# A diffusion layer on one core: one staging tile in another pool, the gate rows loaded earlier, and the mixer's modulation on six tiles with GpSimd and ScalarE beside VectorE

## The chip, the core and the metric

The kernel runs on one core of one Trainium2 chip. The core has TensorE (PE, with its weight loads shown as PEld), VectorE (DVE), ScalarE (ACT), GpSimd (POOL) and SyncE (SP), each with its own instruction stream that runs in order. The metric is the device time of one execution in microseconds. Lower is better.

## The reference

One layer of a diffusion backbone, batch 1, with 256 latent tokens (`LAT`) and 256 context tokens (`CTX`), width 2048, all in float32. The part that matters here:

```python
mod_l = (silu_c @ w_mod[l] + b_mod[l]).reshape(B, N_MOD, D_MODEL)     # 9 modulation vectors of 2048
mod_c = (silu_cc @ w_mod[l] + b_mod[l]).reshape(1, N_MOD, D_MODEL)
xl = half_step_ffn(xl, mod_l, 0, g_norm[l, 0], w_ffn1_up[l], w_ffn1_down[l])   # vectors 0, 1, gate 2
xc = half_step_ffn(xc, mod_c, 0, g_norm[l, 0], w_ffn1_up[l], w_ffn1_down[l])
hl = adaln(xl, g_norm[l, 1], mod_l, 3)                                          # vectors 3, 4
hc = adaln(xc, g_norm[l, 1], mod_c, 3)
# mixer: projections of hl and hc, attention (8 heads, 2 KV heads) and a bidirectional mLSTM (8 heads)
xl = xl + mod_l[:, 5, None, :] * mixer_output(att_l, hm_l, m_l[3], m_gain[l], w_out[l])  # gate 5
xl = half_step_ffn(xl, mod_l, 6, g_norm[l, 2], w_ffn2_up[l], w_ffn2_down[l])    # vectors 6, 7, gate 8
return rms_norm(xl, g_final)

def half_step_ffn(x, mod, i, g, w_up, w_down):
    h = adaln(x, g, mod, i)                       # rms_norm(x, g) * (1 + mod[i+1]) + mod[i]
    a, b = jnp.split(h @ w_up, 2, axis=-1)
    return x + 0.5 * mod[:, i + 2, None, :] * ((jax.nn.silu(a) * b) @ w_down)
```

A modulation vector is a product of one row (the condition) with a 2048 x 2048 weight. `w_mod` has nine of those, 16.8 MB each.

## The kernel before

**Products.** Every float32 weight tile of 128 x 2048 (1 MB) is split into two rounded halves: `hi` by ACT (L102, 128x1024 each) and `lo` by DVE (L103, weight minus `hi`). A product is then three matmuls, `hi*hi`, `hi*lo`, `lo*hi` (`mm3`, L124 to L126). The weight tiles `raw` have three buffers, `hi` and `lo` four of half a tile, that is, two tiles.

**First FFN.** Eleven blocks of 512 hidden columns (`NB`). After the first, each up block is a 2x2 block product by seven products instead of eight (`quad`). Sums of weight tiles that it needs are made by accumulating DMAs into `chain` tiles. Each of the seven has two steps (columns), so a quad has 14 steps of 24 matmuls or more; a step calls `after(step)`. The gated result `ca` is transposed, copied by ACT with a minus sign into a tile `stg` (L670) and stored to HBM by SP (`hid`, L671). `stg`, `ca`, `c12`, `cy`, the two `sraw` tiles and the condition tile `cBh` lie in the pool `f1u`, which is given back after the up products; the pool `f1` with the sums `acc`, the difference tiles and the gate tiles (tag `two`, two buffers) takes its place. `chain` lies in the pool `ch`, which lives until the mixer.

**Down products.** Blocks are taken in pairs (`pair`), again as seven products of two steps each; the last block is done alone (`last1`). In the last pair `through_gate` multiplies finished columns of `acc` by the gate row, vector 2 broadcast over the partitions (L853), and an accumulating DMA of POOL adds the residual. `both_gates` loads the gate rows of both sequences for one column block (L858); they are loaded in the step of their use, for the second, fifth, sixth and seventh product. `last1` loads one gate row per column block and sequence in the same way.

**Modulation.** Vectors 0 and 1 are made on PE at the start. The others are made in units: a unit is a tile of 128 x 1024 weights (0.52 MB, output index on the partitions) times the condition broadcast over the partitions, summed along the row by the same DVE instruction (`mod_half`, L183). A vector has 32 units. `mod_items` paces them: before unit `n` as many steps must have passed as the interpolated `pace` says, plus two (`WAIT`) after each load of a condition half. Vectors 2 to 4 (96 units, two DVE instructions each, for both sequences) run beside the up products of the first FFN. Vectors 5 to 7 (96 units, latent tokens alone) run beside the mixer's projections, in `mod_late`, with two tiles `sraw` that SP loads; vector 8 runs in the second FFN. A step of the mixer is one call of `next(beside["part"])`: one per 128 input rows in `products_of`, one per four in `channels`.

**Mixer.** Weights in order: `w_c`, `w_a`, `w_b` (values and gates), eight `w_mk` heads, eight `w_mq` heads, `w_kv`, `w_q0`, `w_o0`, `w_o1`, `w_q1`, then `w_out`. `conv` (L1168, L1175) follows each head. `latents` builds for each head the masks `E` and the scaled queries `A`; `heads_out` makes `hm`. GpSimd's only products in tiles are `gm` (L1383).

**Order.** The order on each engine is made by a planner from the program order, the dependencies and its estimates; instructions marked by `keep_in_program_order` keep their order among each other. So the same program step may stand earlier or later in another build.

Of the kernel before, what the change touches and what calls it, by code (L numbers as in the profile page):

```python
# [9 lines left out]
F32 = mybir.dt.float32  # L10
F32R = mybir.dt.float32r
BF16 = mybir.dt.bfloat16
# [36 lines left out]
def tile_layer(ctx: ExitStack, tc: tile.TileContext, I: dict, out: bass.AP):  # L49
# [106 lines left out]
    class Conditions:  # L156


        def __init__(self, half, load, at):
            self.half, self.load, self.at = half, load, at  # L160
# [81 lines left out]
    def mod_late(sp, i0, i1, pace):  # L242

        cB = sp.tile([P, 1024], F32, name="cBl", bufs=1)
        cond = Conditions(lambda h: h, lambda h: conditions({LAT: cB}, h, h + 1, (LAT,)), lambda h: {LAT: cB})
        raws = lambda: sp.tile([P, 1024], F32, tag="sraw", name="sraw", bufs=2)
        return mod_items(half_items(i0, i1), nc.sync.dma_start, raws, 2, cond, None, pace)

    def mod_end(i, seqs):

# [51 lines left out]
    def steps(it, n=1):  # L302
        for _ in range(n):
            next(it, None)
# [268 lines left out]
    with pool(name="f1u", bufs=1) as f1u:  # L573
# [87 lines left out]
        def turned():  # L661

            if not turn:
                return
            n, t, ca = turn.pop(0)
            tb = tbank()
            for j in range(FB):
                nc.tensor.transpose(tb[:, j * P : (j + 1) * P], ca[:, j * P : (j + 1) * P], ident)
            stg = f1u.tile([P, CB], F32, tag="stg", name="stg")
            nc.scalar.activation(stg, tb, AF.Copy, scale=-1.0)  # L670
            nc.sync.dma_start(hidd[n][:, t].rearrange("p j c -> p (j c)"), stg)  # L671

# [3 lines left out]
        def c12_tile():  # L676
            return f1u.tile([P, CB], F32, tag="c12", name="c12", bufs=2)
# [84 lines left out]

        halves = [cBh[:, q, :] for q in range(2)]
        cond = Conditions(lambda h: h, lambda h: conditions(halves, h, h + 1), lambda h: halves)
        side = mod_items(half_items(2, 5), nc.sync.dma_start, sraw, 2, cond, lambda: c12_tile().bitcast(BF16), ((96, (NB - 2) * 14 + 2),))

        def first_steps(step):
            if step in (1, 2, 3, 4, 5, 6):
# [86 lines left out]
    def both_gates(cb, seqs=(CTX, LAT)):  # L855
        g = two("gate")
        for s in seqs:
            nc.sync.dma_start(g[:, s, :], mod_rows[2][s, cb * CB : (cb + 1) * CB].partition_broadcast(P))  # L858
        return g

    NP = (NB - 1) // 2

    def pair(p):

        X, Y, Z, ra, gates = {}, {}, {}, {}, None
        w = lambda m, cb: I["w_dn1"][2 * p + m, cb]

        def put(t, cb, b, first=False):
            if first and p == 0:
                nc.scalar.activation(col(t, cb), b, AF.Copy)  # L870
            else:
                nc.vector.tensor_tensor(col(t, cb), col(t, cb), b, op=ALU.add)

        def through_gate(t, cb):

            if p < NP - 1:
                return
            s, tt = divmod(t, 2)
            half_gated(col(t, cb), col(t, cb), gates[:, s, :], -1.0 if cb % 2 else 1.0)
            accum(col(t, cb), xsrc[s][tt * P : (tt + 1) * P, cb * CB : (cb + 1) * CB])  # L880

        def c11x(c, s):
            put(2 * s, 2 * c, X[c, s], True)

        def c11z(c, s):
            put(2 * s, 2 * c, Z[c, s])
            through_gate(2 * s, 2 * c)

        def p5(c, s):
            put(2 * s + 1, 2 * c + 1, Y[c, s], True)  # L890

        def p35(c, s):
            put(2 * s, 2 * c + 1, Y[c, s], True)

# [12 lines left out]

        def loaded(m, cb):
            raw = raw_tile()
            nc.sync.dma_start(raw, w(m, cb))  # L910
            return raw

        def again(c):
            if p + 1 < NP:
                nc.sync.dma_start(chain_[c], I["w_dn1"][2 * p + 2, 2 * c])

        def b22(c):
            ra[c] = loaded(1, 2 * c + 1)
            return ra[c]

        held = lambda c: chain_[c]

        order = (
            ("a11", held, X, True, lambda c: accum(chain_[c], w(0, 2 * c + 1)), c11x, None),
            ("a12", lambda c: loaded(1, 2 * c), Z, True, None, c11z, 0),
            ("n1", held, Y, True, lambda c: accum(chain_[c], w(1, 2 * c + 1)), p5, None),
            ("s4", b22, Y, False, lambda c: accum(ra[c], w(0, 2 * c + 1)), p35, None),
            ("s2", held, X, False, lambda c: accum(chain_[c], w(1, 2 * c)), c12, 1),
            ("s3", lambda c: ra[c], X, False, None, x3, 1),
            ("a22", held, Y, True, again, c21, 0),  # L930
        )
        todo = first_plan if p == 0 else plan if p < NP - 1 else last_plan
        for m, (g, src, dst, fresh, then, use, gate) in enumerate(order):
            a = place0[m] if p == 0 and m < 2 else place[g]
            for c in range(2):
                wt = split(src(c))
                if then:
                    then(c)
                for x in todo.get(2 * m + c, "").split():
                    if x.startswith("raw"):  # L940
                        hid_load(2 * p + 2 + int(x[3]), raws[int(x[3])])
                    else:
                        make[x]()
                if p == NP - 1 and gate is not None:
                    gates = both_gates(2 * c + gate)
                for s in range(2):
                    if fresh:
                        dst[c, s] = tbank() if c and dst is not X else bank()
                    for j in range(FB):
                        k = slice((FB * s + j) * P, (FB * s + j + 1) * P)  # L950
                        mm3(dst[c, s], a[:, 0, k], a[:, 1, k], *wt(slice(j * CB, (j + 1) * CB)), fresh and j == 0, j == FB - 1, True)
                    use(c, s)
# [20 lines left out]
    def last1():  # L973

        norm = iter(())
        kept = {}
        for s in (CTX, LAT):
            for n, cb in enumerate((1, 3, 0, 2) if s == CTX else (2, 0, 3, 1)):
                c = slice(cb * CB, (cb + 1) * CB)
                wt = kept.pop(cb, None) or load_split(I["w_dn1"][NB - 1, cb])  # L980
                if s == CTX and n >= NCB - 2:
                    kept[cb] = wt
                g = both_gates(cb, (s,))[:, s, :]
                for t in range(2 * s, 2 * s + 2):
                    b = bank()
                    block_products(b, wt, t)
                    a = acc[:, t, c]
                    y = f1.tile([P, CB], F32, tag="xr", name="y", bufs=1)
                    half_gated(y, b, g)
                    nc.vector.tensor_tensor(a, a, y, op=ALU.add)  # L990
                    if s == LAT:
                        nc.sync.dma_start(x1d[(t - 2) * P : (t - 1) * P, c], a)
                    if n == 0:
                        ss1[t] = sm.tile([P, 4], F32, tag="ss4", name="ss4", bufs=4)
                    sumsq(ss1[t][:, cb : cb + 1], a)
                    steps(norm, (1, 0, 0, 0, 2, 2, 2, 2)[2 * n + t % 2])
            drain(norm)
            norm = adaln(s)
        return norm
# [32 lines left out]
    with ExitStack() as mx:  # L1032
# [21 lines left out]

        mmcm = pool(name="mm", bufs=1)

        beside["part"] = mod_late(mmcm.__enter__(), 5, 8, ((45, 44), (75, 96), (96, 160)))
        ev_mv(6, 0, b_c)
        b_a = {}
        drain(project("w_a", 416, range(4), b_a))  # L1060
# [13 lines left out]
        def gates():  # L1074
# [35 lines left out]
            for d in range(2):  # L1110
# [15 lines left out]
                nc.vector.tensor_tensor_scan(Mq, uq, uq, m3, ALU.max, ALU.max)  # L1126
                nc.vector.tensor_copy(hc[:, d, 4 + a : 5 + a], m2)
                nc.vector.tensor_tensor(hc[:, d, 4 + z : 5 + z], m2, btT[:, d, 2 + a : 3 + a], op=ALU.add)
            negM = one([NH, 2, T], "negM")
            nc.vector.tensor_scalar(negM, MT.rearrange("h d t q -> h d (t q)"), -1.0, None, op0=ALU.mult)  # L1130
            nc.sync.dma_start(negMd, negM)

# [26 lines left out]


        mkT = one([P, NH, T], "mkT")
        mqT = one([P, NH, T], "mqT")
        C1 = one([P, NH, 2, 130], "C1")

        def conv(b, ch, ns):
# [12 lines left out]
        def state(h, kTc):  # L1178
# [3 lines left out]
                nc.tensor.transpose(tb[:, t * P : (t + 1) * P], kTc[:, t * P : (t + 1) * P], ident)  # L1182
            kn = m1.tile([P, 2, P], F32, tag="kn", name="kn", bufs=1)
            nc.scalar.activation(kn, tb[:, :256].rearrange("p (t d) -> p t d", t=2), AF.Copy)
            vw = m1.tile([P, 2, 2, 130], F32, tag="vw", name="vw", bufs=1)
            for t in range(2):
                for d in range(2):
                    nc.vector.tensor_scalar(vw[:, t, d, :], v1[CTX][:, t, h, :], wg[:, t, d, h : h + 1], None, op0=ALU.mult)
# [36 lines left out]
            todo.append((h, y))  # L1225


        hm = one([P, 2, 1024], "hm")
        ready = [0]

# [551 lines left out]
```

## Time and profile before

| | |
|---|---|
| median of 3 runs | 2760.77 us (2759.16 to 2763.49) |
| the profiled execution | 2753.58 us |
| its span | 2751.9 us |
| mean granted TensorE clock | 0.986 |
| HBM traffic | 234 GB/s over the span |
| modulation units beside the mixer | 96, the first at 1453, the last at 1851 us |
| `lo` splits (L103) of `raw` weights, 128x1024 mostly | 600 of 1205 ns |

Times in the trace are microseconds from the start of the span. A group's line gives its instructions, busy time and mean; an idle engine's time is put down to what ended its wait. The profiled execution is 7.2 us below the median of the timed runs, so differences are worked out against the profile and then carried over to the median.

### The profile page before, as it was taken

What the parts mean: (1) busy time and instruction counts of PE and PEld (TensorE: products, weight loads), DVE (VectorE), ACT (ScalarE), POOL (GpSimd) and SP (SyncE); (2) the same over time, 40 slices, a digit from 0 to 9 for tenths busy, and PEclk for the clock granted to TensorE, in tenths of its full rate; (3) what the DMA queues carried; (4) which work ended last, traced back from release to release, by engine and by line L of the source; (5) the groups of instructions that cost most, each with busy time, mean ns of one, the idle gap of its engine ahead of it and who ended that gap; (6) DMA issues with size and microseconds to landing.
All of it is one profiled execution on the core that took longest, in us unless ns stands there. A gap on an engine that the chain in (4) does not pass through costs nothing. (4 is left out here: it accounts for less than half of the span.)

```text
span 2751.9 us, 33080 instructions
## 1 busy us (share of the span) xinstructions
PE 2647.2 (96%) x12573; PEld 2180.0 (79%) x12573; DVE 1995.5 (73%) x2740; ACT 1263.4 (46%) x1586; POOL 174.6 (6%) x217
## 2 busy tenths in 40 slices
PE   6999999999999889999999998999999999999998
PEld 3588878887878768888789788877898888888886
DVE  2387778778877778888786789797685666666657
ACT  3454444544444455444363335345474444444444
POOL 0000000110000000000210000111000000000000
PEclk8999999999999999999999999999999999999999
DMA  8879999999999969889966766574466666666553
GB/s 349 313 233 249 246 274 277 263 269 268 269 254 266 269 193 239 224 233 219 227 220 217 257 236 234 178 259 161 163 230 227 216 228 223 217 225 225 211 190 132
DMA packets 125887, 645.32 MB, mean 235 GB/s; under 512 B 13464, under 2 KB 17560, under 8 KB 68256
## 3 DMA queue, kind: packets, MB, share of 16 engines
q1 hardware_dynamic: 106144, 513.18, 51.7%
q0 software_dynamic: 19584, 130.03, 24.1%
q8 instruction: 99, 1.62, 0.2%
q14 instruction: 60, 0.49, 0.0%
HBM read 627.36 MB, written 15.79 MB: 234 GB/s over the span
## 5 line engine op out<-in xcount | busy, mean ns | idle before, releaser
L103 DVE TENSOR_TENSOR lo<-raw,hi 128x1024 fp32r<-128x1024 f32 (+3 forms) x600 | 720.3, 1205 | 399.7 <-ACT hi L102 388.4
L102 ACT ACTIVATE hi<-raw 128x1024 fp32r<-128x1024 f32 (+3 forms) x600 | 625.2, 1045 | 796.4 <-PE mm L126 644.5
L125 PE MATMUL mm<-lo,hhi 128*128 128x512 f32 (+3 forms) x1024 | 392.5, 383 | 15.1 <-DVE lo L103 15.0
L124 PE MATMUL mm<-hi,hhi 128*128 128x512 f32 (+3 forms) x1024 | 394.2, 388 | 4.4 <-ACT v L1053 4.4
L126 PE MATMUL mm<-hi,hlo 128*128 128x512 f32 (+3 forms) x1024 | 391.0, 382 | 0.0
L102 ACT ACTIVATE hi<-chain 128x1024 fp32r<-128x1024 f32 x240 | 251.8, 1058 | 264.7 <-PE mm L126 129.5
L103 DVE TENSOR_TENSOR lo<-chain,hi 128x1024 fp32r<-128x1024 f32 x240 | 289.3, 1220 | 98.0 <-ACT hi L102 96.5
L183 DVE SCALAR_TENSOR_TENSOR c<-sraw,cBh 128x1024 bf16<-128x1024 f32 x192 | 229.3, 1218 | 36.8 <-DMA sraw<-in_w_mt 33.5
L124 PE MATMUL mm<-hi,h2hi 128*128 128x512 f32 x640 | 249.1, 389 | 0.0
L125 PE MATMUL mm<-lo,h2hi 128*128 128x512 f32 x640 | 249.0, 389 | 0.0
L126 PE MATMUL mm<-hi,h2lo 128*128 128x512 f32 x640 | 249.0, 389 | 0.0
L125 PEld LDWEIGHTS mm<-lo,hhi 128*128 128x128 f32 x1024 | 195.8, 191 | 51.3 <-DVE lo L103 19.8
L124 PEld LDWEIGHTS mm<-hi,hhi 128*128 128x128 f32 x1024 | 194.5, 190 | 36.6 <-ACT v L1053 4.8
L126 PEld LDWEIGHTS mm<-hi,hlo 128*128 128x128 f32 x1024 | 195.3, 191 | 34.0
L183 DVE SCALAR_TENSOR_TENSOR sraw<-sraw,cBl 128x1024 f32<-128x1024 f32 x128 | 155.6, 1220 | 44.9 <-DMA sraw<-in_w_mt 42.0
L124 PE MATMUL mm<-hhi,hi 128*128 128x512 f32 (+1 forms) x384 | 142.0, 371 | 1.2 <-ACT hi L102 1.2
L124 PEld LDWEIGHTS mm<-hi,h2hi 128*128 128x128 f32 x640 | 120.1, 188 | 25.2
L125 PEld LDWEIGHTS mm<-lo,h2hi 128*128 128x128 f32 x640 | 120.1, 188 | 24.8
L126 PEld LDWEIGHTS mm<-hi,h2lo 128*128 128x128 f32 x640 | 120.1, 188 | 24.8
L126 PE MATMUL mm<-hhi,lo 128*128 128x512 f32 (+1 forms) x384 | 137.9, 361 | 1.2 <-DVE lo L103 1.2
L124 PE MATMUL mm<-hi,hid2h 128*128 128x512 f32 x352 | 138.5, 395 | 0.0
L125 PE MATMUL mm<-hlo,hi 128*128 128x512 f32 (+1 forms) x384 | 138.4, 361 | 0.0
(377 smaller groups left out, 4719.3 us busy)
## 6 DMA issues: line engine op xcount, KB each, us to landing
sraw<-in_w_mt SPq DMA_DIRECT2D x224, 512.0 KB, 5.3
raw<-in_w_up2b SPq DMA_DIRECT2D x80, 1024.0 KB, 4.7
raw<-in_w_dn SPq DMA_DIRECT2D x70, 1024.0 KB, 4.8
chain<-in_w_up1b POOLq DMA_DIRECT2D x60, 1024.0 KB, 11.0
raw<-in_w_up1b SPq DMA_DIRECT2D x40, 1024.0 KB, 8.8
mraw<-in_w_m SPq DMA_DIRECT2D x32, 1024.0 KB, 8.0
chain<-in_w_dn POOLq DMA_DIRECT2D x30, 1024.0 KB, 9.3
chain<-in_w_up1b SPq DMA_DIRECT2D x20, 1024.0 KB, 7.1
```

The source lines that it names most:

```text
L102: nc.scalar.activation(hi, src, AF.Copy)
L103: nc.vector.tensor_tensor(lo, src, hi.bitcast(F32), op=ALU.subtract)
L124: nc.tensor.matmul(out_ap, sh, mh, start=first, stop=False, skip_group_check=skip)
L125: nc.tensor.matmul(out_ap, sh, ml, start=False, stop=False, skip_group_check=skip)
L126: nc.tensor.matmul(out_ap, sl, mh, start=False, stop=last, skip_group_check=skip)
L183: ins = nc.vector.scalar_tensor_tensor(junk() if junk else raw, raw, 1.0, cB[s], op0=ALU.mult, op1=ALU.mult, accum_out=mT[:, i, s, kt, h : ...
```

## The change

Four edits, made together:

1. `stg` moves from `f1u` to `chp`, the pool of `chain`. The tile `y` of `last1`, which had a place in `f1`, uses the same place.
2. The pace of vectors 2 to 4 is `(NB - 2) * 14 - 8` = 118 steps instead of 128 for its 96 units.
3. In the last pair the gate rows are loaded at listed steps (`GATES`), and the sixth product uses the rows of the fifth again; in `last1` the rows of column block `i + 2` are loaded while block `i` is done, into four half tiles.
4. In the mixer the class `Beside` replaces `mod_late`: three tiles of its own and three more that are free until the queries are made (two halves of the place of `mqT`, and the place of `rt`). Units 0 to 71 are "early", and every other of them is multiplied in place by GpSimd and summed by an ACT copy with accumulation; the others stay one DVE instruction. The first six fetches are issued by POOL, all later ones by ACT, one step after a unit's product on DVE or two after one on GpSimd. The pace is 72 units in 54 steps and the other 24 by step 150, instead of 45 in 44, 75 in 96 and 96 in 160. To make room, `negM` shares a place with `nM`, `vw` with `E`, and `mqT` is allocated after the early units are finished.

```diff
+    class Beside:
+        def __init__(self, sp, i0, i1, early, n_early, pace):
...
+            for x in [sp.tile([P, 1024], F32, name=f"sr{j}", bufs=1) for j in range(3)]:
+                self.fetch(x, False, nc.gpsimd)
+            for x in early:
+                self.fetch(x, True, nc.gpsimd)
+        def fetch(self, x, early, queue):
+            if self.asked >= (self.n_early if early else len(self.items)):
+                return
+            i, kt, h = self.items[self.asked]
+            pin(queue.dma_start(x, I["w_mt"][i - 2, kt, :, h * 1024 : (h + 1) * 1024]))
...
+        def one(self):
+            i, kt, h = self.items[self.n]
+            x, early = self.slots[self.n]
+            if self.n < self.n_early and self.n % 2:
+                pin(nc.gpsimd.tensor_tensor(x, x, self.cB, op=ALU.mult))
+                self.due.append((self.done + 2, self.n, True))
+            else:
+                mod_half(x, {LAT: self.cB}, None, i, (LAT,), kt, h)
+                self.due.append((self.done + 1, self.n, False))
+            self.n += 1
+        def finish(self, n, add):
...
+            if add:
+                pin(nc.scalar.activation(x, x, AF.Copy, accum_out=mT[:, i, LAT, kt, h : h + 1]))
+            self.fetch(x, early, nc.scalar)
...
-            stg = f1u.tile([P, CB], F32, tag="stg", name="stg")
+            stg = chp.tile([P, CB], F32, tag="stg", name="stg")
...
-        side = mod_items(half_items(2, 5), ..., ((96, (NB - 2) * 14 + 2),))
+        side = mod_items(half_items(2, 5), ..., ((96, (NB - 2) * 14 - 8),))
...
+    LAST = [(CTX, cb) for cb in (1, 3, 0, 2)] + [(LAT, cb) for cb in (2, 0, 3, 1)]
+    def last_gate(i):
+        if i % 4 in (0, 2) and len(last_gates) < 4:
+            g = two("gate")
+            last_gates.extend((g[:, 0, :], g[:, 1, :]))
+        if i < len(LAST):
+            s, cb = LAST[i]
+            nc.sync.dma_start(last_gates[i % 4], mod_rows[2][s, cb * CB : (cb + 1) * CB].partition_broadcast(P))
...
+        GATES = {0: 0, 1: 2, 4: 1, 5: 3, 11: 0, 12: 2}
...
-                if p == NP - 1 and gate is not None:
-                    gates = both_gates(2 * c + gate)
+                if p == NP - 1:
+                    if (2 * m + c) in GATES:
+                        ahead.append(both_gates(GATES[2 * m + c]))
+                    if 2 * m + c == 13:
+                        last_gate(0)
+                        last_gate(1)
+                    if m in (1, 4, 6):
+                        gates = used[c] = ahead.pop(0)
+                    elif m == 5:
+                        gates = used[c]
...
-                g = both_gates(cb, (s,))[:, s, :]
+                last_gate(i + 2)
+                g = last_gates[i % 4]
...
-                    y = f1.tile([P, CB], F32, tag="xr", name="y", bufs=1)
+                    y = chp.tile([P, CB], F32, tag="stg", name="y")
...
-        beside["part"] = mod_late(mmcm.__enter__(), 5, 8, ((45, 44), (75, 96), (96, 160)))
+        early2 = one([P, 2, 1024], "early2", tag="mqT")
+        mods = Beside(mmcm.__enter__(), 5, 8, [early2[:, 0, :], early2[:, 1, :], one([P, 1024], "early1", tag="rt")], 72, ((72, 54), (96, 150)))
+        beside["part"] = mods.steps()
...
-            negM = one([NH, 2, T], "negM")
+            negM = m1.tile([NH, 2, T], F32, tag="nM", name="negM")
...
-        mqT = one([P, NH, T], "mqT")
...
-            vw = m1.tile([P, 2, 2, 130], F32, tag="vw", name="vw", bufs=1)
+            vw = m1.tile([P, 2, 2, 130], F32, tag="E", name="vw")
...
+        mods.close_early()
+        mqT = one([P, NH, T], "mqT")
```

More of the change, by code (lines that the diff above doesn't have):

```diff
@@ L247, in mod_late, with close_early, steps @@
         return mod_items(half_items(i0, i1), nc.sync.dma_start, raws, 2, cond, None, pace)
+    class Beside:
+        def __init__(self, sp, i0, i1, early, n_early, pace):
+            self.cB = sp.tile([P, 1024], F32, name="cBl", bufs=1)
+            self.items = half_items(i0, i1)
+            self.n_early, self.pace = n_early, pace
+            self.slots = {}
+            self.n = self.done = self.waits = self.asked = 0
+            self.due, self.late = [], []
+            for x in [sp.tile([P, 1024], F32, name=f"sr{j}", bufs=1) for j in range(3)]:
[7 more added lines that the diff above has]
+            pin(queue.dma_start(x, I["w_mt"][i - 2, kt, :, h * 1024 : (h + 1) * 1024]))
+            self.slots[self.asked] = x, early
+            self.asked += 1
+        def one(self):
[9 more added lines that the diff above has]
+        def finish(self, n, add):
+            i, kt, h = self.items[n]
+            x, early = self.slots.pop(n)
+            if add:
+                pin(nc.scalar.activation(x, x, AF.Copy, accum_out=mT[:, i, LAT, kt, h : h + 1]))
+            self.fetch(x, early, nc.scalar)
+            left[i] -= 1
+            if not left[i]:
+                self.late += [(self.done + 2, i, s, v) for s, v in mod_end(i, (LAT,))]
+        def close_early(self):
+            while self.n < self.n_early:
+                self.one()
+            while self.due:
+                self.finish(*self.due.pop(0)[1:])
+        def steps(self):
+            half = None
+            while self.n < len(self.items) or self.due or self.late:
+                while self.n < len(self.items):
+                    h = self.items[self.n][2]
+                    if h != half:
+                        half = h
+                        conditions({LAT: self.cB}, h, h + 1, (LAT,))
+                        self.waits += WAIT
+                    if self.done < np.interp(self.n, *zip((0, 0), *self.pace)) + self.waits:
+                        break
+                    self.one()
+                yield
+                self.done += 1
+                for x in [x for x in self.due if x[0] <= self.done]:
+                    self.due.remove(x)
+                    self.finish(*x[1:])
+                if self.late and self.late[0][0] <= self.done:
+                    mod_rows_out(*self.late.pop(0)[1:])
@@ L249, in mod_end, with pin @@
+    def pin(ins):
+        tc.keep_in_program_order(ins)
     def mod_end(i, seqs):
@@ L764, in tile_layer @@
         cond = Conditions(lambda h: h, lambda h: conditions(halves, h, h + 1), lambda h: halves)
-        side = mod_items(half_items(2, 5), nc.sync.dma_start, sraw, 2, cond, lambda: c12_tile().bitcast(BF16), ((96, (NB - 2) * 14 + 2),))
+        side = mod_items(half_items(2, 5), nc.sync.dma_start, sraw, 2, cond, lambda: c12_tile().bitcast(BF16), ((96, (NB - 2) * 14 - 8),))
         def first_steps(step):
@@ L859, in both_gates @@
         return g
+    LAST = [(CTX, cb) for cb in (1, 3, 0, 2)] + [(LAT, cb) for cb in (2, 0, 3, 1)]
+    last_gates = []
+    def last_gate(i):
[5 more added lines that the diff above has]
+            nc.sync.dma_start(last_gates[i % 4], mod_rows[2][s, cb * CB : (cb + 1) * CB].partition_broadcast(P))
     NP = (NB - 1) // 2
     def pair(p):
-        X, Y, Z, ra, gates = {}, {}, {}, {}, None
+        X, Y, Z, ra = {}, {}, {}, {}
+        gates = None
         w = lambda m, cb: I["w_dn1"][2 * p + m, cb]
@@ L921, in pair @@
         held = lambda c: chain_[c]
+        GATES = {0: 0, 1: 2, 4: 1, 5: 3, 11: 0, 12: 2}
+        ahead, used = [], {}
         order = (
[L924 to L930, printed above, removed]
+            ("a11", held, X, True, lambda c: accum(chain_[c], w(0, 2 * c + 1)), c11x),
+            ("a12", lambda c: loaded(1, 2 * c), Z, True, None, c11z),
+            ("n1", held, Y, True, lambda c: accum(chain_[c], w(1, 2 * c + 1)), p5),
+            ("s4", b22, Y, False, lambda c: accum(ra[c], w(0, 2 * c + 1)), p35),
+            ("s2", held, X, False, lambda c: accum(chain_[c], w(1, 2 * c)), c12),
+            ("s3", lambda c: ra[c], X, False, None, x3),
+            ("a22", held, Y, True, again, c21),
         )
         todo = first_plan if p == 0 else plan if p < NP - 1 else last_plan
-        for m, (g, src, dst, fresh, then, use, gate) in enumerate(order):
+        for m, (g, src, dst, fresh, then, use) in enumerate(order):
             a = place0[m] if p == 0 and m < 2 else place[g]
@@ L977, in last1 @@
         for s in (CTX, LAT):
-            for n, cb in enumerate((1, 3, 0, 2) if s == CTX else (2, 0, 3, 1)):
+            for i, (_, cb) in [(i, x) for i, x in enumerate(LAST) if x[0] == s]:
+                n = i % NCB
                 c = slice(cb * CB, (cb + 1) * CB)
```

## The prediction

> **What bounds the kernel now.** First the page: how busy each engine is, and where TensorE is not.
>
> ```profile
> span 2751.9 us, 33080 instructions
> ...
> PE 2647.2 (96%) x12573; PEld 2180.0 (79%) x12573; DVE 1995.5 (73%) x2740; ACT 1263.4 (46%) x1586; POOL 174.6 (6%) x217
> ...
> PE   6999999999999889999999998999999999999998
> ```
>
> TensorE is the bound almost everywhere: 2647.2 of 2751.9 us. An edit pays only where PE idles, or where it runs at half clock after idling. So I next read a table of the stretches that the diff touches (columns: busy time and instructions of PE, PEld, DVE, ACT, POOL; then granted clock, DMA share, GB/s).
>
> ```profile
> 954.00:1012.00 58.00, 43.42 (x173) 33.18 (x172) 42.77 (x54) 24.64 (x30) 1.75 (x2) 0.91 0.57 178
> 1359.00:1378.00 19.00, 12.75 (x47) 9.36 (x47) 16.50 (x22) 4.29 (x5) 6.75 (x8) 0.91 0.93 242
> 1457.00:1645.00 188.00, 176.09 (x837) 155.34 (x836) 133.99 (x252) 57.44 (x89) 1.97 (x4) 0.95 0.73 251
> 1645.00:1725.00 80.00, 69.34 (x512) 65.98 (x512) 73.30 (x181) 45.47 (x63) 2.22 (x4) 0.96 0.68 231
> 1725.00:1865.00 140.00, 134.31 (x638) 109.84 (x636) 113.66 (x240) 58.04 (x80) 26.52 (x32) 0.99 0.60 208
> ```
>
> PE idles 14.6, 6.3, 11.9, 10.7 and 5.7 us there: 49 of its 105 idle us. The stretches are the hand-over from the first FFN's up products to its down products, the gates, and three parts of the mixer (w_a, w_b and the eight w_mk heads; w_mq; w_kv to w_o1). The waits say what ends last (waiter, released by: us, times, longest). Over the whole span:
>
> ```profile
> ACT acc L870 <- DMA hid<-stg: 9.7, 1, 9.7
> ...
> DVE acc L853 <- DMA gate<-mod: 8.6, 3, 7.4
> ```
>
> DVE's own in 1457 to 1645:
>
> ```profile
> DVE sraw L183 <- DMA sraw<-in_w_mt: 36.0, 23, 4.2
> DVE sraw L183 <- DMA cBl<-ccd: 2.4, 1, 2.4
> ```
>
> All are waits for transfers, in engines that run strictly in order, with the `hi` (L102) and `lo` (L103) splits of the next weights queued behind them. PE then waits for `lo`.
>
> An idle stretch also costs clock. One row right after the gates' stall:
>
> ```profile
> 1374.10:1377.40 3.30, 3.30 (x9) 2.58 (x8) 3.00 (x4) 0.04 (x1) 1.08 (x2) 0.50 0.60 152
> ```
>
> PE works, at half clock, for 3.4 us, which loses 1.7. The idle pieces before it were 2.67, 0.67 and 2.91 us. [...]
>
> **Part by part**, against the profiled execution (2753.58 us, span 2751.9).
>
> *Staging tile in the lasting pool.* Before, `stg` lies in the pool that `acc` and the difference tiles replace, so ACT's first `acc` copy (9.65 us idle) and DVE's first `v` (8.28 us idle) both wait until 994 for the last store of `stg`. Behind them stand the splits. PE's gaps that follow are 3.49 + 0.95 + 2.02 + 0.63 + 0.40 + 0.64 = 8.1 us, and a half-clock stretch from 998.6 loses 1.7. After, the last users of that space are the transposes of `ca`, done at 983. Late next is DVE's own backlog (16 us of splits and differences), which starts 8.3 us earlier. Taken **-9** (bounds -10 and -5, if the backlog alone still makes half the gaps).
>
> *Pace of the second to fourth modulations* (128 steps become 118). The last two-tile fetches no longer fall at 944 to 974. There DVE waits 6.1 us for `sraw`, PE 6.09 us for `lo` behind it, and 6.8 us at half clock lose 3.4: -9.5. In exchange 8% more units per step run before. Between 150 and 954 the same kind of wait costs PE 10.1 us and 1.7 of clock, with the DMA share at 0.97. I add 3 (bounds 0 and 9.5). Net **-6.5** (-9.5 to 0).
>
> *Gates.* The gate rows of the middle products now go out at steps 4 and 5 and are used at 8 and 9, some 22 us later (a step is 24 matmuls, 5.4 us), against a median landing of 5.2 us; four of 16 loads vanish. Gone: 2.67 + 0.67 + 2.91 of PE, and 1.7. The last pair's go out one step ahead, about a landing, so a little can stay; the SP queue behind them holds only `w_dn` loads that have three buffers. The gates of the last block are two deep, 11 us ahead. Taken **-7** (-8 to -3).
>
> *The mixer up to the end of w_mk* (188 us now). PE's floor there: 188 - 11.9 idle - 9.4 of clock (5%) = 167. Counted in the two built programs' orders, DVE does 39 modulation units up to there instead of 56, GpSimd 36 and ACT 36 sums. DVE: 134 - 17 x 1.22 = 113 us. GpSimd's price is not shown for 128x1024; its 128x512 product is the nearest row, with ACT's rows above and below it left out:
>
> ```profile
> L1383 POOL TENSOR_TENSOR gm<-gm,mg x4: 1297/1704/2197, 1827.0 to 1862.0; 128x512 f32<-128x512 f32 x4
> ```
>
> Undisturbed 1.30 us: twice is 2.6, and 2.4 if the smallest POOL instruction (0.19) is its fixed part. I take 2.5: 36 x 2.5 = 90 us. What that costs DVE stands in the timeline (first POOL, then DVE):
>
> ```profile
> 1830.48 1.68 POOL L1383 TENSOR_TENSOR gm<-gm,mg 128x512 f32<-128x512 f32 x1
> ...
> 1830.94 2.30 DVE L103 TENSOR_TENSOR lo<-raw,hi 128x1024 fp32r<-128x1024 f32 x1
> ```
>
> The split that usually takes 1.22 took 2.30: it ended 1.2 us after the product did, so it stood still while the product ran. A reduction with one input next to the product at 1826.95 kept its 0.67. [...]
>
> So the stage lies between 167 (all products under waits and one-input work: -21) and 113 + 90 = 203 (none: +15); with all 38 us of DMA waits kept as well, 241 (+53). The blocked split is the nearest row, so I cover little: half of the 30 us, and 13 us of landing waits that I expect to stay (six tiles instead of two, but 18 more units of 0.52 MB raise the DMA share from 0.73 to about 0.87). DVE: 113 + 90 - 28 + 13 = 188, plus 2 for unevenness. Stage 190: **+2**.
>
> ACT's load is 57 + 36 x 1.24 (a 1.05 pass and a 0.19 accumulator read) + 66 DMA issues x 0.33 (SP's row) = 124 us: fits. But each sum now waits for a product and each refetch for DVE, with `hi` queued behind; DVE and PE wait for that `hi`. SP loses 80 fetches that stood between weight loads: nothing for PE, whose weights have three buffers.
>
> *w_mq* (80 us): here DVE is the bound (73.3). Units fall from 17 to 7, -12.2; 12 mask instructions of 0.28 come in from the stage before, +3.4: 64.5, under PE's floor of 80 - 10.7 - 3.2 = 66. But its gaps are the chain from `mqT` through the masks to `hm`, which keeps its length. **-7** (-14 to 0). *w_kv to w_o1*: 23 units become 14; idle 5.7 and clock 1.4: **-2** (-5 to 0).
>
> At nothing: `vw`, `negM`, `mqT` in shared tiles. Their earlier holders end a stage before (early units at w_mk's end), and if not, `mqT` waits with 66 us of w_mq behind it, which is in the slow rival.
>
> Sum: -9 - 6.5 - 7 + 2 - 7 - 2 = -29.5: 2753.6 becomes 2724.1. The median of the runs lies 7.2 above the profiled time: **2731**.
>
> **Rivals.** *GpSimd is hidden.* DVE idles 38 us for landings in this stage; if most products fall there, it goes to about 170 (-18), w_mq to -10, the rest to -3: -53.5, **2707**. For it: the waits are as many us as a good part of the products. Against: the blocked split.
>
> *Six tiles don't speed the fetch.* Refetches sit in ACT's queue behind `hi`, which waits 91 us for PE in this stage (45.7 + 45.0). If DVE's 38 us of landing waits stay, the stage is 113 + 62 + 38 = 213 (+25) instead of 190: **2754**, about no change. This is also the case where the change doesn't do what it says.
>
> *The chain over three engines, slower.* DMA, GpSimd, ACT's sum, ACT's issue, `hi`: every product uncovered and the waits kept, 241 us (+53 instead of +2): **2782**. It decides from a stage of 219.5 us (the other terms give -31.5), that is (219.5 - 113) / 36 = 3.0 us of DVE standstill per product, landing waits in it. For it: POOL's products stretch to 2.2 us per 512 when they meet DVE. Against: four of them stretched DVE by 1.1 only. [...]
>
> **Numbers.** Forecast 0.42, hidden 0.25, no faster fetch 0.15, slower chain 0.18. A measurement of this kernel tells about 0.2% (5.5 us) from no change: 2755.3 and 2766.3. Faster: 0.42 + 0.25 + half of 0.15 = 0.75. Same: the rest of 0.15 and 0.02 of the chain's: 0.09. Slower 0.16. The range goes from the hidden case to the upper part of the third: 2707 to 2764; some 0.06 lies below and 0.14 above.
>
> **What would show it.** No PE gap over 1 us near 985 to 1000, none at the last up block's end, none at the gates. In the mixer: POOL products of 2.4 to 3.5 us, `lo` often 2 to 3.5 us instead of 1.22, DVE's waits for landings at a third, the stage near 190. Wrong if `lo` stays at 1.22 (hidden), or if ACT waits for POOL over 40 us there (chain), or if new gaps between 150 and 920 eat the hand-over's gain.

## The result and the profile after

The changed kernel takes 2776.41 us (median of four executions, 2770.62 to 2778.52) against 2759.97 us for the kernel before (2757.32 to 2763.49). The ratio is 1.0055, with a 95% interval of 1.0036 to 1.0075: it is slower, where 2731 was forecast. The profiled execution took 2776.03 us, with a span of 2774.0, 22.1 us more than the span before. The page's head and its row of TensorE's busy tenths:

```profile
span 2774.0 us, 33029 instructions
...
PE 2657.3 (96%) x12573; PEld 2185.5 (79%) x12573; DVE 2010.4 (72%) x2668; ACT 1308.0 (47%) x1664; POOL 275.7 (10%) x259
...
PE   6999999999999999999998689999999999999998
```

The dips at the hand-over (894 to 1032 us) and in `w_mq` (1651 to 1720) are gone from the row; the gaps at the gates were too short to make a dip there. A deeper one is new, 8, 6 and 8 in the slices from 1456 to 1664 us, in the mixer. The table of the same stretches shows it (busy time of PE, PEld, DVE, ACT, POOL; then clock, DMA share, GB/s); the third row is the stage from the last values of `w_c` to the last `w_mk` head, the fourth `w_mq`:

```profile
954.00:1012.00 58.00, 56.15 (x254) 45.70 (x252) 38.71 (x39) 33.61 (x41) 3.50 (x4) 1.00 0.85 236
1359.00:1378.00 19.00, 19.00 (x85) 15.67 (x85) 17.00 (x23) 8.15 (x8) 4.71 (x6) 1.00 1.00 246
1454.00:1685.00 231.00, 189.61 (x837) 162.27 (x837) 171.00 (x217) 95.12 (x156) 97.24 (x38) 0.89 0.72 255
1685.00:1750.00 65.00, 64.15 (x500) 62.27 (x499) 60.15 (x160) 50.81 (x72) 4.54 (x8) 1.00 0.57 191
```

The first two rows and the last are nearly full, at clock 1.00. The stage is not: PE idles 41.4 us in it, at a mean clock of 0.89. Marks that both kernels have (the last copy into `stg`, the first copy into `acc`, the first gated sum, and so on) split the 22.1 us:

| stretch | before | after | difference |
|---|---|---|---|
| start to the last `stg` copy | 982.9 | 999.4 | +16.5 |
| to the first `acc` copy | 11.2 | 0.5 | -10.7 |
| to the first `through_gate` | 314.2 | 315.4 | +1.2 |
| gates, to the last `y` | 119.8 | 110.3 | -9.5 |
| last `y` to the values of `w_c` | 28.2 | 28.2 | 0 |
| the stage to the last `w_mk` head | 188.6 | 230.9 | +42.3 |
| `w_mq` | 78.2 | 65.3 | -12.9 |
| `w_kv` to `w_o1` | 138.2 | 133.3 | -4.9 |
| the rest | 890.6 | 890.7 | +0.1 |

Two things cost: the mixer's stage, and the up products of the first FFN. The stage's groups on DVE and POOL (count, busy time and mean in ns, then idle time before them), first two of the kernel before, then those of the changed one:

```profile
L183 DVE SCALAR_TENSOR_TENSOR sraw<-sraw,cBl 128x1024 f32<-128x1024 f32 x54 | 65.6, 1222 | 38.9 <-DMA sraw<-in_w_mt 36.0 <-DMA cBl<-ccd 2.4
L103 DVE TENSOR_TENSOR lo<-raw,hi 128x1024 fp32r<-128x1024 f32 x19 | 23.1, 1219 | 9.5 <-PE mm L1192 6.3 <-ACT hi L102 3.2
```

```profile
L183 DVE SCALAR_TENSOR_TENSOR sr<-sr,cBl 128x1024 f32<-128x1024 f32 x21 | 41.1, 1961 | 17.5 <-DMA sr<-in_w_mt 17.5
L103 DVE TENSOR_TENSOR lo<-raw,hi 128x1024 fp32r<-128x1024 f32 x19 | 33.7, 1788 | 1.7 <-ACT hi L102 1.7
L183 DVE SCALAR_TENSOR_TENSOR early<-early,cBl 128x1024 f32<-128x1024 f32 x18 | 29.6, 1651 | 10.1 <-DMA early<-in_w_mt 10.1
```

```profile
L279 POOL TENSOR_TENSOR early<-early,cBl 128x1024 f32<-128x1024 f32 x18 | 49.0, 2721 | 38.2 <-DMA early<-in_w_mt 38.2
L279 POOL TENSOR_TENSOR sr<-sr,cBl 128x1024 f32<-128x1024 f32 x18 | 47.9, 2661 | 67.2 <-DMA sr<-in_w_mt 58.4 <-DMA cBl<-ccd 8.6
```

GpSimd's products take 2.69 us on average. VectorE's units, 1.22 us before, now take 1.65 to 1.96 on average, and `lo` takes 1.79 instead of 1.22. PE waits 23.9 us for `lo` and 7.0 us for `hi` in the stage, where it waited for neither before. The timeline shows the meeting itself (start, duration); first POOL, whose line holds two products, then DVE:

```profile
1558.16 6.72 POOL L279 TENSOR_TENSOR sr<-sr,cBl 128x1024 f32<-128x1024 f32 x2
```

```profile
1562.55 3.41 DVE L183 SCALAR_TENSOR_TENSOR early<-early,cBl 128x1024 f32<-128x1024 f32 x1
1565.89 0.08 DVE L183 DVE_READ_ACCUMULATOR early<-early,cBl 128x1 f32 x1
1565.89 1.21 DVE L103 TENSOR_TENSOR lo<-raw,hi 128x1024 fp32r<-128x1024 f32 x1
```

The products end at 1564.88. The unit that started at 1562.55 ends at 1565.96, 1.1 us later, which is nearly its own length. It stood still until GpSimd was done. The whole stage bears this out: of VectorE's 58 units and `lo` splits of 128x1024, 20 started while a product ran, and these took 1.62 to 3.43 us; the other 38 took 1.23 at most. Six of the 20 were `lo`, which does not read the condition's tile, so it isn't that both engines read this tile.

VectorE's waits in the stage (waiter, released by: us, times, longest):

```profile
DVE sr L183 <- DMA sr<-in_w_mt: 17.5, 8, 7.6
DVE C L1296 <- PE mm L1295: 16.7, 4, 7.0
DVE early L183 <- DMA early<-in_w_mt: 10.1, 2, 5.5
DVE gv L188 <- ACT early L290: 4.8, 1, 4.8
DVE lo L103 <- ACT hi L102: 4.7, 3, 2.3
```

So DVE is busy 171 us, close to the 175 of the prediction's working, but idles 60 us beside it, where the prediction left 15. Waits for fetched tiles to land (`sr` and `early`) are 27.6 of the 60; the wait for PE at `C`, 16.7, was 0.3 before.

### The profile page after: what moved, and what is told of

Its sections match the earlier page's. It is cut to its first block, busy times and chain, and to the rows that moved or that the text cites. A ratio compares the mean times of both kernels' runs of the same rounds, so it can differ in the third digit from the quotient of the medians.

```text
span 2774.0 us, 33029 instructions
## 1 busy us (share of the span) xinstructions
PE 2657.3 (96%) x12573; PEld 2185.5 (79%) x12573; DVE 2010.4 (72%) x2668; ACT 1308.0 (47%) x1664; POOL 275.7 (10%) x259
## 3 DMA queue, kind: packets, MB, share of 16 engines
q8 instruction: 99, 1.62, 0.2%
## 5 line engine op out<-in xcount | busy, mean ns | idle before, releaser
L103 DVE TENSOR_TENSOR lo<-raw,hi 128x1024 fp32r<-128x1024 f32 (+3 forms) x600 | 737.2, 1235 | 392.0 <-ACT hi L102 389.2
L125 PE MATMUL mm<-lo,hhi 128*128 128x512 f32 (+3 forms) x1024 | 395.6, 386 | 27.6 <-DVE lo L103 27.5
L126 PE MATMUL mm<-hi,hid2l 128*128 128x512 f32 x352 | 137.0, 390 | 0.0
```

The source lines that it names most:

```text
L103: nc.vector.tensor_tensor(lo, src, hi.bitcast(F32), op=ALU.subtract)
L125: nc.tensor.matmul(out_ap, sh, ml, start=False, stop=False, skip_group_check=skip)
L126: nc.tensor.matmul(out_ap, sl, mh, start=False, stop=last, skip_group_check=skip)
```

## The experiments

In all tables below, "stage" is the time from the values of `w_c` to the last `w_mk` head, and "idle" is the stage less DVE's busy time in it, from the profiled execution. Times are medians, ratios are against the kernel before on the same chip. There were two chips: the half columns, the one input, the mixer's edit alone and the last kernel ran on the second, all others here on the first; between chips, compare the ratios.

### Undoing one part at a time

**The old pace in the changed kernel**

```diff
- mod_items(half_items(2, 5), ..., ((96, (NB - 2) * 14 - 8),))
+ mod_items(half_items(2, 5), ..., ((96, (NB - 2) * 14 + 2),))
```

> The changed kernel with the pace of vectors 2 to 4 put back to 128 steps; all else as changed. Pace theory: the up products lost some 16 us because 8% more units per step make VectorE wait more often for a two-tile fetch with a split queued behind it; so about 2760 us (16 below the changed kernel), the last store of stg near 983 us instead of 999, VectorE's waits for sraw there back from 53 to some 34 us. Rival (the pace is harmless, the moved staging tile changed the order or the loads of the up products): about 2776 us and the last stg copy still near 999.

2766.14 us, ratio 1.0023 (1.0007 to 1.0039). The stage is 232.2, as in the changed kernel, so it keeps that loss. The new pace cost some 10 us instead of gaining 6.5.

**Staging tile and gates alone**, on the kernel before: edits 1 and 3 of the change, nothing else.

> The kernel before with two of the edits alone: the staging tile in the lasting pool and the gate rows loaded ahead. Old pace, old mixer. If both work as the stage times of the two traces say (-10.7 us at the hand-over, -9.5 us at the gates): about 2740 us, PE gaps over 1 us gone near 985 to 1012 and at the gates. Rival (the move of stg is what cost the up products 16 us): about 2755 us.

2739.52 us, ratio 0.9916 (0.9884 to 0.9948): 20 us gained. These two edits do what was forecast (-9 and -7), if not a little more.

**No GpSimd in the mixer**

```diff
-            if self.n < self.n_early and self.n % 2:
+            if False:
```

Every early unit is one DVE instruction; GpSimd's products and ACT's sums are gone, the six tiles stay.

> The changed kernel with all early units as one VectorE instruction: no product on GpSimd, no sum on ScalarE; six tiles, fetches by ScalarE and all paces as changed. Port theory (a GpSimd product stops VectorE): the stage from w_a to the last w_mk goes from 231 to about 190 us, the run to some 2737 us. Rival (what costs is that fetches sit in ScalarE's queue and 72 units come in 54 steps): stage 215 to 230 us, 2762 to 2776 us.

2733.03 us, ratio 0.9910 (0.9877 to 0.9942): 43 us below the changed kernel. VectorE does 36 units more there, and the stage is still 42 us shorter.

**GpSimd's products over 32 columns**

```diff
-                pin(nc.gpsimd.tensor_tensor(x, x, self.cB, op=ALU.mult))
+                pin(nc.gpsimd.tensor_tensor(x[:, :32], x[:, :32], self.cB[:, :32], op=ALU.mult))
```

Only 32 of 1024 columns are multiplied; the waits, sums, fetches and the order of the instructions stay.

> The changed kernel with GpSimd's product over the first 32 of the 1024 columns alone (the other columns stay unmultiplied); every instruction, wait, sum and fetch is kept in its place. Port theory: VectorE's units and splits return from 1.65 to 1.96 us each to 1.22, its busy time in the stage from 171 to about 113 us, the stage from 231 to 185 to 195 us, the run to some 2735 us. Chain theory (GpSimd, ScalarE's sum, ScalarE's issue, hi in one line): the stage stays over 215 us and the run over 2760, for the chain is as long as before less 2.5 us per product. Were both at work, in between.

2740.62 us, ratio 0.9939 (0.9916 to 0.9963). All hops between DMA, GpSimd, ACT and DVE (each waits for the one before) are still there; only the length of the products went, and 36 us with it. The two kernels' rows of the stage, without GpSimd and with short products:

```profile
1457.30:1646.40 189.10, 173.66 (x838) 152.01 (x837) 154.94 (x289) 69.27 (x99) 0.93 (x2) 0.97 0.85 311
```

```profile
1450.70:1648.40 197.70, 175.80 (x836) 153.25 (x835) 116.45 (x217) 94.99 (x155) 16.58 (x38) 0.95 0.81 296
```

With short products DVE has 38 us less to do than without GpSimd, and the stage is 8.6 us longer. The hops have a price of their own: PE waits 18.5 us for `lo` and `hi` here, and 2.6 us for `lo` without GpSimd.

### Is it the standstill, the hops or the queue?

The changed kernel was run again on the first chip, beside three others: the refetches by SP, and two of the later sections (the new pace alone, and no GpSimd with the old pace).

> The changed kernel as it is, on one chip with the three kernels below, so that single edits are read against it. From its first four executions 2776 us; its median here between 2770 and 2781, 0.5% above the kernel before. If it comes out below 2766, the difference of 10 us that I put down to the pace (128 steps became 118) was chance.

2775.5 us (six executions, 2773.06 to 2778.41), ratio 1.0052 (1.0034 to 1.0070): the loss repeats.

**Refetches issued by SP instead of ACT**

```diff
-            self.fetch(x, early, nc.scalar)
+            self.fetch(x, early, nc.sync)
```

> The changed kernel, but the refetches of the modulation's tiles are issued by SP instead of ACT. Rival (the tiles are fetched late because each refetch stands in ACT's queue behind `hi`): DVE's 28 us of landing waits between w_c's end and the last w_mk head mostly go, the stage falls from 231 to about 205 and the time to about 2750. Theory (VectorE stands still while GpSimd multiplies, whoever fetches): DVE's busy time there stays at 165 to 175 us, single units at 1.6 to 2.0 us, the stage at 222 to 235 and the time at 2766 to 2781. SP's stream also holds the weight loads, so that a wait for a slot can hold those up: above 2781 if it does.

2767.93 us (2759.84 to 2777.17), ratio 1.0024 (1.0007 to 1.0041): 7.6 us less, on the same chip. The waits show why it is not more:

```profile
DVE lo L103 <- ACT hi L102: 20.1, 9, 8.9
DVE sr L183 <- DMA sr<-in_w_mt: 12.2, 5, 7.6
DVE lo L103 <- PE mm L1295: 8.5, 3, 3.8
...
DVE early L183 <- DMA early<-in_w_mt: 1.9, 1, 1.9
```

The landing waits fall from 34.4 us in the repeat (27.6 in the first profile) to 14.1, but a wait for `hi` of 20.1 us takes their place. DVE is still busy 165.9 us, its idle time is 59.5, and the stage is 225.4. ACT's queue looks like a small part of the price. The run gives no more than a rough size, because the planner ordered this program otherwise: 421 of DVE's 2668 instructions stand at another place.

**GpSimd's products over half the columns**: as above with 512 in place of 32; the other half isn't multiplied.

> The changed kernel, but GpSimd multiplies only 512 of the 1024 columns of its units (the other half isn't multiplied); waits, sums and fetches stay. If VectorE's standstill is the price, it goes with the length of the product: products of about 1.3 us, VectorE's busy time up to the last w_mk head at about 144 us, halfway between 116 (32 columns) and 171 (1024), the stage at 207 to 220 and the time about halfway between 2740.6 and 2775.5, at 2752 to 2764. If it is the chain of hops over three engines, which is as long here as with 32 columns: 2741. If it is a threshold (below it the products hide in waits): 2741 too, but with units at 1.4 us or more.

2747.70 us, ratio 0.9948 (0.9930 to 0.9967). The products take 1.57 us (about 1.3 was expected), but DVE's busy time is 130.0, the stage 201.7 and the run 2747.7, all below what the theory of a proportional standstill said (144, 207 to 220, 2752 to 2764). By the ratios the first half of the columns costs 0.0009 of the run, which is within the noise, and the second half 0.0104, or 29 us. The traces show why it is not proportional: with 512 columns 15 of VectorE's 58 units and splits started inside a product and lost 0.55 us each; with 1024 columns 20 did and lost 1.72 us each. So both the number of meetings and the loss of each grow with the length.

**A one-input instruction on GpSimd**

```diff
-                pin(nc.gpsimd.tensor_tensor(x, x, self.cB, op=ALU.mult))
+                pin(nc.gpsimd.tensor_scalar(x, x, 1.0, None, op0=ALU.mult))
```

> The changed kernel, but GpSimd's 36 instructions take one input of 128x1024 and multiply it by 1.0, in place of the product with the condition's tile (so these units aren't multiplied by it); the order of all instructions is the same. If VectorE stands still only for products with two inputs: units and `lo` back at 1.22 us, VectorE's busy time near 116 us in the stage, the time at 2741 like the kernel with 32 columns. If it stands still beside any instruction of GpSimd over so many columns: units above 1.6 us and 2755 to 2776, by the duration of the instruction.

2745.45 us, ratio 0.9945 (0.9926 to 0.9965). This is the sharpest comparison, because the order of all instructions is the changed kernel's and GpSimd is even busier than in it, 110.7 us of the stage against 97.4 (POOL and then DVE):

```profile
L279 POOL TENSOR_SCALAR sr<-sr 128x1024 f32<-128x1024 f32 x18 | 57.8, 3210 | 46.6 <-DMA sr<-in_w_mt 46.6
L279 POOL TENSOR_SCALAR early<-early 128x1024 f32<-128x1024 f32 x18 | 52.4, 2913 | 24.1 <-DMA early<-in_w_mt 24.0
```

```profile
L183 DVE SCALAR_TENSOR_TENSOR sr<-sr,cBl 128x1024 f32<-128x1024 f32 x21 | 27.8, 1330 | 29.0 <-DMA sr<-in_w_mt 29.0
L183 DVE SCALAR_TENSOR_TENSOR early<-early,cBl 128x1024 f32<-128x1024 f32 x18 | 24.4, 1362 | 18.9 <-DMA early<-in_w_mt 18.8
```

The instruction takes 3.06 us, longer than the product, and ACT idles 30 us ahead of its sums (40 in the changed kernel). Yet DVE's units take 1.33 to 1.36 us on average and 30 us of the run come back. Of VectorE's 58 units and splits of 128x1024, 33 started while a one-input instruction ran; 21 of them took no more than 1.23 us, the others up to 2.05. So it is not that GpSimd is slow; it is that its product with two inputs stops VectorE. The runs side by side (standstill is DVE's busy time in the stage over that with 32 columns, divided by 36):

| GpSimd's instruction | its time | DVE busy | standstill each | idle | stage | run |
|---|---|---|---|---|---|---|
| product, 32 columns | 0.44 | 116.5 | 0 | 81.2 | 197.7 | 2740.6 |
| one input, 1024 | 3.06 | 125.2 | 0.24 | 80.2 | 205.4 | 2745.5 |
| product, 512 | 1.57 | 130.0 | 0.38 | 71.7 | 201.7 | 2747.7 |
| product, 1024 | 2.69 | 171.0 | 1.52 | 59.9 | 230.9 | 2776.4 |
| none (DVE alone) | | 154.9 | | 34.2 | 189.1 | 2733.0 |

### The mixer's edit alone, and the pace alone

**The mixer's edit alone**, on the kernel before: edit 4 of the change.

> The kernel before with the mixer's edit alone (staging tile, gates and pace stay old). From the marks of the changed kernel, which loses 25 us between the end of w_c and the end against the kernel before: +25, about 2786. By the prediction's terms (+2, -7, -2): 2754.

2780.51 us, ratio 1.0079 (1.0050 to 1.0107): 20 us slower. That is all that the staging tile and the gates gain.

**The new pace alone**, on the kernel before.

> The kernel before with the pace of vectors 2 to 4 alone changed, from 128 to 118 steps. By the prediction -6.5 us (the waits for the last two-tile fetches at 944 to 974 go): 2753. By the first comparison +10: 2770, with DVE's waits for `sraw` between 150 and 985 at 60 us or more instead of 49 (33.5 and 15.7), and the gap at 954 not smaller. Without an effect: 2760. Here the staging tile still stops the down products, so a part of either can vanish in that wait.

2761.95 us, ratio 1.0007 (0.9993 to 1.0021): no difference. Part of the cost comes back at the hand-over: the last `stg` copy starts at 999.4 instead of 982.9, but the first `acc` copy follows after 5.5 us instead of 11.2. Where `stg` lies in the lasting pool it follows after 0.5 to 1.4 us, so there is nothing left to shrink. That this is why the pace costs its full price there is argued, not shown, for single profiles differ at this mark by as much.

Two pairs of kernels with `stg` in the lasting pool differ by the pace alone: the changed kernel with the old pace and as it is, and the kernel without GpSimd with the old pace (next section) and the new. In both the new pace brings the last `stg` copy later, 999.4 against 987.9 and 1001.3 against 989.5. One stretch where it loses is 150 to 500 us, here of the kernel before and of the changed one:

```profile
150.00:500.00 350.00, 347.44 (x1558) 286.63 (x1557) 282.42 (x340) 170.07 (x193) 30.19 (x34) 1.00 0.92 250
```

```profile
150.00:500.00 350.00, 341.09 (x1509) 279.87 (x1509) 278.02 (x336) 162.13 (x186) 29.25 (x33) 0.99 0.91 248
```

PE is busy 6.4 us less in the same time. This holds in every profile of the study, whatever else the kernel changes. In the six with 128 steps PE's busy time in this stretch is 346.0 to 348.2 us, in the eight with 118 it is 339.0 to 343.3; DVE's waits for `sraw` in it are 5.3 to 10.4 us in the former and 12.1 to 20.3 in the latter. In the two pairs the new pace costs PE 9.4 and 9.0 us of busy time from 150 to 850 us. It also costs clock there: TensorE runs at half clock for 20.5 us with the new pace in both, against 0 and 6.8 us with the old, which loses another 10.2 and 6.8 us of work. From 940 to 1020, where the last fetches no longer fall, PE gains 3.2 and 5.0 us of busy time and 3.4 us of clock.

### The best combination

**No GpSimd and the old pace**: staging tile, gates and six tiles on DVE alone, 128 steps.

> The changed kernel without GpSimd's products and ACT's sums (each early unit is one VectorE instruction) and with the old pace of 128 steps for vectors 2 to 4; staging tile, gates and six tiles stay. If the newer pace costs what the first comparison says (2776.4 against 2766.1), this is 10 us below the 2733 of the kernel with the new pace: about 2723. If the pace does what the prediction said (6.5 us gained by the new one): 2740. If it is worth nothing: 2733.

2724.87 us (2723.93 to 2726.45), ratio 0.9867 (0.9848 to 0.9886): the fastest kernel of the study, 51 us below the changed one and about 36 below the one before. Against the kernel without GpSimd and with the new pace it gains 8 us, which is the price of the pace a second time. Its stage and its `w_mq`:

```profile
1442.20:1633.92 191.72, 176.15 (x836) 153.55 (x835) 155.32 (x289) 69.28 (x98) 0.88 (x2) 0.96 0.83 307
1633.92:1697.42 63.50, 62.91 (x499) 61.25 (x497) 58.50 (x154) 47.87 (x65) 5.26 (x8) 1.00 0.56 195
```

The stage is 6.3 us longer than with two tiles (185.4, staging tile and gates alone), for 75 units instead of 54, and `w_mq` is 13.2 us shorter (76.7 there).

**The same with refetches by SP**

> The fastest kernel so far (staging tile, gates and six tiles, no GpSimd, old pace: 2724.9) with refetches issued by SP instead of ACT. If ACT's queue delays the fetches, VectorE's 23 us of landing waits in the stage up to the last w_mk head shrink to about 10 and the time falls by about 5, to 2720. If SP's weight loads now wait behind the fetches: the same or up to 2730.

2727.55 us, ratio 0.9878 (0.9857 to 0.9899): no gain. DVE's landing waits fall from 25.4 to 9.2 us and the stage from 191.7 to 184.2, as expected, but `w_mq` takes 69.5 us instead of 63.5. The gain is given back one stage later. Here too the planner's order differs, at 453 of DVE's 2740 instructions, so this is no test of the queue alone.

## Why the prediction was wrong

**Staging tile: right.** Forecast -9 (-10 to -5); the time between the last `stg` copy and the first `acc` copy fell by 10.7 us, a little beyond the bound.

**Gates: right.** Forecast -7 (-8 to -3); -9.5 measured, also beyond the bound, with no PE gap and no half clock left from 1359 to 1378. The term had counted 1.7 us of lost clock, from the row at 0.50 (1374.1 to 1377.4); the stretch from 1359 to 1378 is at 1.00 now and was at 0.91 before.

**Pace: wrong, and the sign with it.** Forecast -6.5, as -9.5 for the waits at 954 and +3 for 8% more units per step. The -9.5 nearly came true: 6.6 and 8.4 in the two pairs of kernels that differ by the pace alone (940 to 1020 us). The +3 is the term that failed: from 150 to 850 us the new pace lost 19.6 and 15.8, about half of it clock, and the waits for `sraw` between 150 and 500 doubled (7.5 to 16.2 us, 6.1 to 12.8). These are single profiles; by the medians the step costs 9.4 us (2775.5 against 2766.1) and 8.2 (2733.0 against 2724.9), and nothing that the run shows where the staging tile still stops the down products. The bound of 9.5 on the +3 would have made it zero, so even that end was too small. The profile before also flattered the up products: its last `stg` copy came at 982.9, and those of the five other profiles with 128 steps at 987.9 to 999.8. So the +16.5 of the first table is partly that one execution.

**The mixer's stage: wrong, and this decides the sign.** Forecast +2, measured +42.3. The terms for VectorE's own work came out: products of 2.69 us for 2.5, 97 us of them for 90, DVE's busy time 171 for 175 (113 + 90 - 28). The sum is in part luck, for the base was 116 and 42 us of the products were covered, not 28. Of the 28, 15 are "half of the 30 us", a term that no run shows; of VectorE's other work in the stage `conv`'s 28 instructions kept their 0.74 us, and `vw` went from 0.28 to 0.39. The blocked split from which the standstill was read ended 1.08 us after its product by the rows shown, not 1.2; nothing hangs on it. What failed is the next term: "13 us of landing waits that I expect to stay", plus 2 for unevenness. DVE idled 54.1 us in this stage before; the sum let 39 of it vanish, and 60 stayed. The landings were 27.6 of it, not 13, and the sum had no term for DVE's new waits, 16.7 us for PE at `C` and 4.8 for ACT's sums at `gv`. The floor of 167, at which all products would be hidden, has the same mistake: with 32 columns and DVE at 116 us the stage is 197.7, and the shortest stage of any kernel here is 184.2. Of the 41 us that were missed, 31 are there without the long products (197.7 against 167) in the hops, the landing waits and the other idle time, which no run splits further, and 10 lie in the cover (the long products add 33, and 190 less 167 is 23).

**The rivals.** The slow chain (241, 2782) came nearest: 231 and 2776, beyond its point of decision of 219.5. Its mechanism was only partly right. ACT did idle 40 us ahead of its sums, about what the rival's sign asked, but mostly for VectorE's units (30 us), and for POOL 4.7. Nor were all products uncovered: they cost DVE 55 of their 97 us. So it is not the chain as it was written; it is the standstill, with all of the idle time kept. "Hidden" is excluded by the stage itself (231 us against about 170) and by `lo` at 1.79. "Six tiles don't speed the fetch" is half right: with GpSimd 27.6 us of landing waits stay; without it, 24 to 25 (waits for `cBl` with them) against 38, for some 20 units more.

**`w_mq`: mis-sized, -12.9 for -7.** The chain from `mqT` to `hm` was thought to keep its length. With 10 units fewer in DVE's queue it did not, within the term's bounds: PE is busy 64.15 of 65 us. *`w_kv` to `w_o1`*: -4.9 for -2, at the end of its bounds.

Without GpSimd the kernel is 43 us faster. That its product takes 2.69 us, and a unit on VectorE 1.22, is not the main cause, as the one-input run with its 3.06 us shows; the standstill is, with some 30 of the 43 us; no run splits the rest.

## What to carry to other kernels

Price a second engine's instruction by what it stops as well as by what it takes over: here each GpSimd product freed VectorE of 1.22 us and cost it 1.52, so VectorE gained nothing by it. Do not set a stage equal to one engine's busy time when that engine idled over a quarter of it before; keep the idle time in the sum unless the very wait is removed, and show which. And test bundled edits apart: two good ones (-20 us together) were hidden by one bad one, and an edit that cost nothing beside a stall cost 8 to 9 us once the stall was gone.

## What the runs showed of the hardware

A GpSimd product with two inputs, 128x1024 in f32, takes 2.33 us at the least and 2.69 on average beside VectorE, and VectorE's units and `lo` splits of 128x1024, with two such inputs, take 1.62 to 3.43 us instead of 1.22 when they start during it. That is 20 of 20 in the changed kernel's trace and 20 of 23 in its repeat, where the other three took 1.21 within one product of 8.9 us. The product is longer beside VectorE as well: the two of the timeline took 6.72 us together, where twice 2.33 is 4.66. With half the columns the cost to VectorE is a quarter, 0.38 us for each product instead of 1.52. A one-input GpSimd instruction over the same tile takes 2.77 us and more, so it is not faster, but VectorE's units in its kernel stay at 1.33 to 1.36 us on average. The instruction costs VectorE 0.24 us, against 1.52 for the product. Why it costs so much less, and why 12 of the 33 instructions that met it took longer all the same, stays open: no run looked at shorter pieces or other operations. "Port theory" is the author's name for the standstill; no run shows a port, only these times.
